# In-projection of a convolution layer by halves of the tokens instead of all at once: gate weights loaded twice, two quarters normalised in between

## The chip, the core and the metric

One core of a Trainium2 chip runs the whole program. It has a tensor engine (PE, with its weight loads as PEld), a vector engine (DVE), a scalar engine (ACT), GpSimd (POOL) and a queue that issues loads (SP). Each engine works through its own instructions in the order in which the program issued them, and waits at semaphores for others. The metric is the device time of one execution in microseconds (us).

## The reference, cut to what matters

One inference step over 1024 prompt tokens and 8 sample tokens, 1024 features, two layers. The change touches the first half of layer 0, a pair of convolutions:

```
up = rmsnorm(hp, g[0])                       # over 1024 features of each token
a_val, a_gate, b_x, b_gb, b_gc = split_cols(up @ w_in, [512, 512, 512, 512, 512])
ga = a_val * sigmoid(a_gate)                 # A: 31-tap depthwise convolution over tokens
ya = silu(layernorm(dwconv_valid(ga, a_w) + a_b, a_ln_g, a_ln_b))
zb = b_gc * b_x                              # B: 3-tap convolution
yb = b_gb * dwconv_valid(zb, b_w)
y = concatenate([ya, yb]) @ w_out
hp = hp + rmsnorm(y, g[1])                   # post-norm, then pre-norm and the MLP
```

Behind it come the MLP, the attention layer and a second MLP, none of which the change touches.

## The kernel before, in words

Features lie on partitions and tokens on the free axis. Tokens come in blocks of 512, 256 and 264 (`BW`): block 0 is the first half, blocks 1 and 2 the second. For the input norm block 0 is taken as two quarters of 256 tokens, and blocks 1 and 2 are the third and the fourth quarter (`quarters`).

All products run in a split form: a float32 operand x is kept as h, its rounding to the type fp32r, and l = x - h. ACT casts h, DVE (or POOL) subtracts l (`split_later`). A product takes three matmuls: h with h, h with l, l with h (`project`). A weight tile of 128 output columns is loaded as `raw`, 512 KB, and split into two tiles `w` (`Weights.split`); eight slices of 128 features make 24 matmuls per tile and block. `net.splitter` is the engine that subtracts: POOL from the start of the convolution layer until the first half is projected, then None, which stands for DVE; the first weights of each list go to DVE in any case.

The norm of a quarter (`normaliser`): ACT squares pieces of x, DVE adds them up (`total`), PE sums over partitions with a matrix of ones (`st`, a float32 matmul that the trace shows as two instructions), ACT takes the root, DVE refines it in three `newton` steps. Then `scaled`, for each of eight slices: DVE multiplies x by gain and root (`norm`, into PSUM), ACT casts `xh`, DVE subtracts `xl`.

The first convolution, A: for each of four chunks c of 128 channels, `glu` projects the gate g and the value v, ACT takes the sigmoid into `ga`, DVE multiplies by v. When a pair of chunks is there for a half, the task `taps` runs 31 taps for each on DVE (`taps` in PSUM in the first half, `cv` in SBUF in the second). `norm` is the layer norm behind it, whose first ones matmul is `mean`. The second, B: `conv_b(hf, c)` projects three tiles (x, c, b), and DVE and ACT do the three taps on `z`. When all of B and the layer norm of a half are there, `half` projects it with the output weights `woc` (`mm<-ybh` and `mm<-yah`), post-norms it (`y`), and pre-norms it for the MLP. These tasks run beside the main order; the MLP of the first half begins when its `xn` is there and the main order has ended the layer.

What stands in which order on an engine is decided when the program is built: the main order in `conv_layer` issues matmuls, a planner (`Pace`) keeps an estimate of each engine's time, and tasks (norms, splits, taps, half) issue their next instructions when that estimate has passed their due time. `pace.wait` lets tasks run until a condition holds. `Weights` keeps the load order (`weight_order`); `limit` is how many tiles may be loaded ahead, `ahead` how many may be split ahead of the one in use.

The main order before: chunks 0 and 1 of A for each of the four quarters in turn, the weights held; then chunks 2 and 3 of A for all three blocks; then B of the first half; then B of the second half.

Of the kernel before, what the change touches and what calls it, by code (L numbers as in the profile page):

```python
# [22 lines left out]
NB = 3  # L23
OFF = (0, 512, 768)
BW = (512, 256, 264)
KP = (2, 4, 4)
HALVES = ((0,), (1, 2))
# [28 lines left out]
LN_EXP = "natural_log_exp_and_others"  # L56
# [170 lines left out]
class Weights:  # L227
# [30 lines left out]
    def split(self, i, x, n):  # L258
        net = self.net
        yield net.pace.ready(x) + 0.1  # L260
        while i - self.taken >= self.ahead:
            yield net.pace.now() + 0.3
        h = yield from net.unit_later("w", F32R, self.back)
        l = yield from net.unit_later("w", F32R, self.back)
        yield from net.split_later(h[:, :n], l[:, :n], x[:, :n], net.splitter if i > 1 else None)
        net.free(x)
        self.whole -= 1
        self.cut.add(i)
        self.ready[i] = (h, l)
# [105 lines left out]
class Net:  # L375
# [31 lines left out]
    def weight_order(self):  # L407
        io = self.io
        main, back = [], []
        wic = lambda *cs: main.extend((io["wic"][c], 1024) for c in cs)  # L410
        wic(4, 0, 5, 1, 6, 2, 7, 3)
        for _ in range(2):
            for c in range(4):
                wic(8 + c, 16 + c, 12 + c)
        for i in range(2):
            for hf in range(2):
                for ch in range(NF // 4):
                    if i and hf and 0 < ch < NF // 4 - 1:
                        w = lambda r, c: io["w1"][i, 4 * ch + 2 * r:4 * ch + 2 * r + 2, :, c * 512:(c + 1) * 512]
                        main.append((tuple(w(r, c).rearrange("f p c -> p f c") for r in range(2) for c in range(2)), 1024))  # L420
                    else:
                        main.extend((io["w1"][i, 4 * ch + f], 1024) for f in range(4))
                    main.extend((io["w2"][i, 4 * ch + f], 1024) for f in range(4))
        for hf in range(2):
            back.extend((io["woc"][c], 1024) for c in range(KD))
        for hf in range(2):
            back.extend((io["wv"][j], 4 * NW) for j in range(2))
            back.extend((io["wia"][c], 1024) for c in (4, 0, 1, 2, 3, 11, 5, 6, 7, 8, 12, 9, 10))
            back.extend((io["woa"][c], 768) for c in range(KD))
        return main, back  # L430
# [92 lines left out]
        yield self.pace.soon()  # L523
        (engine or self.dve).tensor_sub(l, x, raw(h))

    def rstd(self, r, total, n, w, urgent, follows=LN_EXP):
        if urgent:
            bank = yield from self.bank_later("st")
            ps = bank[:, :w]
            self.pe.matmul(ps, lhsT=self.ones, rhs=total[:, :w], start=True, stop=True)  # L530
        else:
            u = yield from self.unit_later("st", F32R)
            parts = u[:, :w], u[:, SMALL:SMALL + w]
            yield from self.split_later(*parts, total[:, :w])
            yield self.pace.soon()
            bank = yield from self.bank_later("st")
            ps = bank[:, :w]
            for i in range(2):
                self.pe.matmul(ps, lhsT=self.ones_r, rhs=parts[i], start=i == 0, stop=i == 1)
            self.free(u)  # L540
        r = r[:, :w]
        self.table(LN_EXP)
        yield self.pace.soon()
        self.table(LN_EXP)
        self.act.activation(r, ps, AF.Ln, bias=self.eps, scale=1.0 / n)
        self.act.activation(r, r, AF.Exp, scale=-0.5)
        at = self.pace.soon()
        self.table(follows)
        yield at
        t = self.tmp(w, name="newton")  # L550
        self.dve.scalar_tensor_tensor(t, ps, float(n * EPS), r, ALU.add, ALU.mult)
        self.dve.scalar_tensor_tensor(t, t, -0.5 / n, r, ALU.mult, ALU.mult)
        self.dve.scalar_tensor_tensor(r, t, 1.5, r, ALU.add, ALU.mult)
        self.banks.give(bank)

    def normaliser(self, x, n, w):

        total = yield from self.small("total")
        m = x[0].shape[1]
        view = lambda t: t[:, :m * w].rearrange("p (m t) -> p m t", m=m)  # L560
        self.act.square(view(total), x[0])
        before = None
        for a in x[1:]:
            s = yield from self.small("sq")
            self.act.square(view(s), a)
            at = self.pace.soon()
            if before is not None:
                self.dve.tensor_add(view(total), view(total), view(before))
                self.drop(before)
            before = s  # L570
            yield max(at - 0.5, self.pace.calm())
        yield at
        self.dve.tensor_add(view(total), view(total), view(before))
        self.drop(before)
        if m == 2:
            self.dve.tensor_add(total[:, :w], total[:, :w], total[:, w:2 * w])
        yield self.pace.ready(total)
        r = yield from self.small("rstd")
        yield from self.rstd(r, total, n, w, self.urgent)
        self.drop(total)  # L580
        return r

    def root(self, sums, urgent):
# [432 lines left out]
    def conv_layer(self, post, first_done):  # L1016
        pace, io, sm, W = self.pace, self.io, self.small_const, self.W
        xn = [None] * NB
        quarters = [(0, slice(0, 256)), (0, slice(256, 512)), (1, slice(0, 256)), (2, slice(0, 264))]
# [21 lines left out]
            xl.append(self.feat(b, KD, "xl", F32R))  # L1041
        sa_unit, sb = self.unit("sa"), self.const.tile([P, 4, NS, 2], F32, name="sb")
        sa = sa_unit[:, :4 * NS * 30].rearrange("p (c b j) -> p c b j", c=4, b=NS)
        self.pool.dma_start(out=sa, in_=io["sa"])
        self.pool.dma_start(out=sb, in_=io["sb"])
        normed = []

        scaling = []

        def norm_in(i):  # L1050
            b, c = quarters[i]
            w = c.stop - c.start
            while i > 1 and len(scaling) < i:
                yield pace.now() + 0.2
            yield pace.ready(*x[i].tiles) if i else 0.0
            r = self.normaliser(self.pieces(x[i]), 1024, w)
            r = yield from r
            while i == 1 and not normed:
                yield pace.now() + 0.2
            scaling.append(i)  # L1060
            parts = yield from self.scaled(x[i], xh[b], xl[b], range(KD), 0, r[:, :w], c)
            self.drop(r)
            yield from self.all(parts)
            self.free(*x[i].tiles)
            normed.append(c)
# [213 lines left out]

        pace.spawn(half(0))  # L1280
        ws = []
        for i, quarter in enumerate(quarters):
            pace.wait(lambda: len(normed) > i)
            for c in range(2):
                if i == 0:
                    ws += [W.get(), W.get()]
                    W.limit = 3
                    W.ahead = 2
                glu(c, *quarter, ws[2 * c], ws[2 * c + 1], i == 0)
        for w in ws:  # L1290
            W.done(w)
        for c in (2, 3):
            wg, wv = W.get(), W.get()
            for b in range(NB):
                glu(c, b, slice(0, BW[b]), wg, wv)
            W.done(wg)
            W.done(wv)
        for hf in range(2):
            for c in range(4):
                conv_b(hf, c)  # L1300
            for b in HALVES[hf]:
                self.free(*xh[b].tiles, *xl[b].tiles)
            self.splitter = None
            projected[hf] = True
        self.pool.dma_start(out=io["o_bp"], in_=tail)
        self.pool.dma_start(out=io["o_bs"], in_=new_bs)
# [710 lines left out]
def build(tc, io):  # L2017
    with ExitStack() as ctx:
        ctx.enter_context(tc.manual_schedule())
        net = Net(ctx, tc, io)  # L2020
        net.attn_setup()
        res = [net.dr.tile([P, KD * T], F32, name=f"res{i}") for i in range(3)]
        xn = [[None] * NB for _ in range(3)]
        net.conv_layer(net.junction(1, 2, io["x"], res[0], xn[0]), lambda: xn[0][0])
        net.operands(xn[0], 0)
        net.back = BACK
        net.pace.spawn(net.carry_caches())
        gate = lambda b: xn[0][2] if b == 0 else xn[2][0]
        after = [net.junction(3, 4, res[0], res[1], xn[1], gate), net.junction(7, None, res[2], io["o_y"], None)]
        join = net.junction(5, 6, res[1], res[2], xn[2], summed=True)  # L2030
        net.urgent = False
        for hf in range(2):
            net.mlp(hf, xn[0], after[0])
            net.pace.spawn(net.attn(hf, xn[1], join))
        for hf in range(2):
            end = net.mlp(hf, xn[2], after[1], hf == 1, hf == 1)
        net.pace.wait(lambda: end.done)
# [114 lines left out]
```

## Time and profile before

| | us |
|---|---|
| median of 3 runs | 2199.3 (2199.19 to 2201.35) |
| the profiled execution | 2196.17 |
| its span in the profile | 2194.4 |

The profile is of one execution, which lies 3.1 us below the median; its span leaves 1.8 us of that execution outside. All stretches below are counted from the start of the span. A matmul's duration in the trace is modelled and overlaps its neighbours, so the pace of matmuls is read from the distance between the events that they release. PEclk is the granted clock of PE as a share of full speed (2.4 GHz); half of it is 1.2 GHz.

### The profile page before, as it was taken

The numbers are of one execution on the slowest core, as the hardware profiler recorded it, in microseconds if no ns is written. First come the engines' busy times: TensorE is split into PE (matmuls) and PEld (weight loads), VectorE is DVE, ScalarE is ACT, GpSimd is POOL, SyncE is SP. The second block draws the span as 40 slices with busy tenths as digits, with TensorE's granted clock in tenths as the row PEclk, the third lists the DMA queues.
The fourth block names the chain that finished last, engine by engine and source line by source line (L and its number), as shares of the span: only waits on it lengthen the run. The fifth ranks groups of instructions, "written<-read, shape, count | busy, mean of one in ns | idle before, by whom it ended". The sixth has DMA issues, their size and how long they took to land. (4 is left out here: it accounts for less than half of the span.)

```text
span 2194.4 us, 35516 instructions
## 1 busy us (share of the span) xinstructions
PE 2147.5 (98%) x13895; PEld 1947.7 (89%) x13895; DVE 1566.1 (71%) x2889; ACT 1113.2 (51%) x2245; POOL 149.9 (7%) x256
## 2 busy tenths in 40 slices
PE   5999999999999999999999999999999999999997
PEld 4987898889888998999989989988887989999997
DVE  8886588984764756788649575767876487777756
ACT  6125344345453643788555364356875455545434
POOL 2132010010000011000000001201000000000000
PEclk9999999999999999999999999999999999999999
DMA  4112544353533345233343343433333344232241
GB/s 180 49 58 96 166 177 157 96 173 97 174 106 117 125 154 168 85 107 119 117 142 125 123 143 124 156 121 129 103 104 125 122 166 143 107 118 86 87 140 55
DMA packets 88616, 271.04 MB, mean 124 GB/s; under 512 B 16937, under 2 KB 19129, under 8 KB 88265
## 3 DMA queue, kind: packets, MB, share of 16 engines
q1 hardware_dynamic: 77744, 223.70, 31.0%
q0 software_dynamic: 10704, 45.08, 5.4%
q8 instruction: 109, 1.79, 0.3%
q14 instruction: 59, 0.48, 0.1%
HBM read 235.41 MB, written 45.37 MB: 128 GB/s over the span
## 5 line engine op out<-in xcount | busy, mean ns | idle before, releaser
L77 PE MATMUL mm<-xh,w 128*128 128x264 f32 (+2 forms) x4208 | 997.4, 325 | 3.8 <-DVE xl L77 3.1
L77 PEld LDWEIGHTS mm<-xh,w 128*128 128x128 f32 x4208 | 710.4, 189 | 69.6 <-DVE xl L77 3.3
L77 PE MATMUL mm<-hid,w 128*128 128x264 f32 (+2 forms) x4608 | 750.7, 321 | 0.0
L77 PEld LDWEIGHTS mm<-hid,w 128*128 128x128 f32 x4608 | 658.1, 188 | 65.2 <-issue 2.7
L77 PE MATMUL mm<-xl,w 128*128 128x264 f32 (+2 forms) x2104 | 678.7, 323 | 0.0
L77 DVE TENSOR_TENSOR w<-raw,w 128x1024 fp32r<-128x1024 f32 (+1 forms) x348 | 418.5, 1210 | 173.7 <-ACT w L77 173.1
L77 ACT CAST w<-raw 128x1024 fp32r<-128x1024 f32 (+1 forms) x368 | 375.0, 1035 | 153.8 <-DMA raw<-w 58.6
L77 PEld LDWEIGHTS mm<-xl,w 128*128 128x128 f32 x2104 | 398.4, 189 | 31.3 <-issue 1.0
L77 DVE TENSOR_TENSOR acc<-acc,mm 128x256 f32<-128x256 f32 (+2 forms) x336 | 164.4, 508 | 98.8 <-PE mm L77 97.2
L77 ACT ACTIVATE relu<-mm 128x256 f32<-128x256 f32 (+2 forms) x192 | 87.3, 455 | 266.3 <-PE mm L77 238.8
L77 DVE TENSOR_TENSOR hid<-mm,hid 128x256 fp32r<-128x256 f32 (+2 forms) x192 | 97.8, 513 | 136.2 <-ACT hid L77 135.2
L77 ACT ACTIVATE mm<-relu 128x256 f32<-128x256 f32 (+2 forms) x192 | 88.8, 462 | 6.1
L77 ACT ACTIVATE hid<-relu 128x256 fp32r<-128x256 f32 (+2 forms) x192 | 91.3, 475 | 0.0
L77 DVE SCALAR_TENSOR_TENSOR cv<-ga,small,cv 128x512 f32<-128x512 f32 x120 | 83.3, 746 | 0.0
L77 DVE SCALAR_TENSOR_TENSOR taps<-ga,small,taps 128x482 f32<-128x482 f32 (+29 forms) x120 | 78.7, 734 | 0.0
L77 PE MATMUL mm<-xt,w 128*128 128x264 f32 x576 | 73.6, 284 | 0.7 <-DVE w L77 0.7
L77 PEld LDWEIGHTS mm<-xt,w 128*128 128x128 f32 x576 | 71.3, 188 | 1.3 <-DVE w L77 1.3
L77 ACT COPY qk<-mm 128x512 f32<-128x512 f32 (+2 forms) x39 | 17.4, 447 | 106.2 <-PE mm L77 101.3
L77 ACT COPY y<-mm 128x512 f32<-128x512 f32 (+2 forms) x48 | 21.5, 447 | 91.6 <-PE mm L77 91.6
L77 DVE TENSOR_TENSOR sq<-sq 128x264 f32<-128x264 f32 (+2 forms) x84 | 43.2, 514 | 30.6 <-ACT sq L77 29.7
L77 PE MATMUL mm<-mixh,w 128*128 128x512 f32 (+2 forms) x288 | 64.9, 320 | 0.0
L77 ACT CAST ph<-pt 128x512 fp32r<-128x512 f32 (+1 forms) x80 | 41.2, 523 | 34.8 <-PE pt L77 32.3
(259 smaller groups left out, 2288.6 us busy)
## 6 DMA issues: line engine op xcount, KB each, us to landing
raw<-w SPq DMA_DIRECT2D x256, 512.0 KB, 3.9
raw<-wic SPq DMA_DIRECT2D x32, 512.0 KB, 4.6
raw<-wia SPq DMA_DIRECT2D x26, 512.0 KB, 3.6
res<-res SPq DMA_DIRECT2D x18, 512.0 KB, 4.6
raw<-woc SPq DMA_DIRECT2D x16, 512.0 KB, 3.7
o_d_s<-c_d POOLq DMA_DIRECT2D x8, 1023.5 KB, 17.3
qscr<-qk POOLq DMA_DIRECT2D x26, 256.0 KB, 2.3
res<-y POOLq DMA_DIRECT2D x12, 512.0 KB, 3.8
```

Of the source, the lines that this page charges most:

```text
L77: r = fn(*args, **kw)
```

## The change

The main order now runs chunks 0 and 1 of A for the first two quarters, chunks 2 and 3 of A for block 0, B of the first half; then all four chunks of A for blocks 1 and 2, and B of the second half. The eight weight tiles of A are thus loaded and split twice. No weights are split ahead until the first two quarters have been issued (`ahead` is 0, then 0, then 2). The third and fourth quarters begin their norm only when `later` is set, behind the first two quarters. The second quarter's sum of squares is made on PE alone: two ones matmuls for each squared piece (`pe_normaliser`). DVE splits the first four weights instead of two. POOL stays the splitter through the second half's projection. Attention's constants are set up after the convolution layer is issued.

```diff
@@ Weights.split
-        yield from net.split_later(h[:, :n], l[:, :n], x[:, :n], net.splitter if i > 1 else None)
+        yield from net.split_later(h[:, :n], l[:, :n], x[:, :n], net.splitter if i > 3 else None)
@@ weight_order
-        wic(4, 0, 5, 1, 6, 2, 7, 3)
         for _ in range(2):
+            wic(4, 0, 5, 1, 6, 2, 7, 3)
             for c in range(4):
                 wic(8 + c, 16 + c, 12 + c)
@@ rstd
-        if urgent:
+        if bank is not None:
+            ps = bank[:, :w]
+        elif urgent:
@@ new
+    def pe_normaliser(self, x, n, w):
+        bank = yield from self.bank_later("st")
+        for i, a in enumerate(x):
+            s = yield from self.small("sq")
+            self.act.square(s[:, :2 * w].rearrange("p (m t) -> p m t", m=2), a)
+            yield self.pace.soon()
+            for m in range(2):
+                self.pe.matmul(bank[:, :w], lhsT=self.ones, rhs=s[:, m * w:(m + 1) * w], start=i + m == 0,
+                               stop=i == len(x) - 1 and m == 1)
+            self.drop(s)
+        r = yield from self.small("rstd")
+        yield from self.rstd(r, None, n, w, True, bank=bank)
+        return r
@@ conv_layer, norm_in
-            while i > 1 and len(scaling) < i:
+            while i > 1 and (len(scaling) < i or not later):
                 yield pace.now() + 0.2
             yield pace.ready(*x[i].tiles) if i else 0.0
-            r = self.normaliser(self.pieces(x[i]), 1024, w)
-            r = yield from r
+            r = yield from (self.pe_normaliser if i == 1 else self.normaliser)(self.pieces(x[i]), 1024, w)
@@ conv_layer, main order
-        for i, quarter in enumerate(quarters):
+        for i, quarter in enumerate(quarters[:2]):
             pace.wait(lambda: len(normed) > i)
             for c in range(2):
                 if i == 0:
                     ws += [W.get(), W.get()]
                     W.limit = 3
-                    W.ahead = 2
+                    W.ahead = 0
                 glu(c, *quarter, ws[2 * c], ws[2 * c + 1], i == 0)
+            W.ahead = 2 * i
         for w in ws:
             W.done(w)
-        for c in (2, 3):
-            wg, wv = W.get(), W.get()
-            for b in range(NB):
-                glu(c, b, slice(0, BW[b]), wg, wv)
-            W.done(wg)
-            W.done(wv)
+        later.append(True)
+        self.pool.dma_start(out=sa, in_=io["sa"])
+        self.pool.dma_start(out=sb, in_=io["sb"])
         for hf in range(2):
+            for c in (range(4) if hf else (2, 3)):
+                wg, wv = W.get(), W.get()
+                for b in HALVES[hf]:
+                    pace.wait(lambda: len(normed) > b + 1)
+                    glu(c, b, slice(0, BW[b]), wg, wv)
+                W.done(wg)
+                W.done(wv)
             for c in range(4):
                 conv_b(hf, c)
             for b in HALVES[hf]:
                 self.free(*xh[b].tiles, *xl[b].tiles)
-            self.splitter = None
+            self.splitter = None if hf else self.splitter
             projected[hf] = True
@@ build
-        net.attn_setup()
         res = [net.dr.tile([P, KD * T], F32, name=f"res{i}") for i in range(3)]
         xn = [[None] * NB for _ in range(3)]
         net.conv_layer(net.junction(1, 2, io["x"], res[0], xn[0]), lambda: xn[0][0])
+        net.attn_setup()
```

The order in which instructions stand on an engine shows three places. First, PE at the very start of the program, before the change (`st` are ones matmuls, `mm` projections; xN is a count of like rows):

```order
L2148 UNCONDITIONAL_BRANCH
L77 MATMUL st<-total,ones 128x256 x2
L77 MATMUL mm<-xh,w 128x256
L77 MATMUL mm<-xl,w 128x256
L77 MATMUL mm<-xh,w 128x256 x2
L77 MATMUL mm<-xl,w 128x256
```

and with the change:

```order
L2165 UNCONDITIONAL_BRANCH
L77 MATMUL st<-total,ones 128x256
L77 MATMUL st<-sq,ones 128x256 x8
L77 MATMUL mm<-xh,w 128x256
L77 MATMUL mm<-xl,w 128x256
```

The second quarter's single `st` on DVE's total has become eight on ACT's squares, still ahead of the first projection.

Second, PE where the third quarter's `st` stands. Before, it is inside the first quarter's projection, 58 matmuls behind the start:

```order
L77 MATMUL mm<-xl,w 128x256
L77 MATMUL mm<-xh,w 128x256
L77 MATMUL st<-total,ones 128x256
L77 MATMUL mm<-xh,w 128x256
L77 MATMUL mm<-xl,w 128x256
```

With the change it stands behind both quarters' chunks 0 and 1, three matmuls into the gate of chunk 2:

```order
L77 MATMUL mm<-xh,w 128x256
L77 MATMUL mm<-xh,w 128x512
L77 MATMUL mm<-xl,w 128x512
L77 MATMUL mm<-xh,w 128x512
L77 MATMUL st<-total,ones 128x256
L77 MATMUL mm<-xh,w 128x512
```

Third, DVE where the adds of that quarter stand (`ga` is the product of gate and value). Before, they are among the norms of the second quarter:

```order
L77 SCALAR_TENSOR_TENSOR norm<-x,small,rstd 128x256 x2
L77 TENSOR_TENSOR total<-total,sq 128x512
L77 SCALAR_TENSOR_TENSOR norm<-x,small,rstd 128x256
L77 TENSOR_TENSOR total<-total,sq 128x512 x2
L77 TENSOR_TENSOR total<-total 128x256
```

With the change they stand behind three of the four products of the first two quarters and among the first taps:

```order
L77 TENSOR_TENSOR xl<-norm,xh 128x256 x3
L77 TENSOR_TENSOR ga<-mm,ga 128x256 x3
L77 TENSOR_SCALAR taps<-ga,small 128x512 x2
L77 SCALAR_TENSOR_TENSOR taps<-ga,small,taps 128x482 x2
L77 TENSOR_TENSOR total<-total,sq 128x512
L77 SCALAR_TENSOR_TENSOR taps<-ga,small,taps 128x483
L77 TENSOR_TENSOR total<-total,sq 128x512
L77 SCALAR_TENSOR_TENSOR taps<-ga,small,taps 128x483
L77 SCALAR_TENSOR_TENSOR taps<-ga,small,taps 128x484
L77 TENSOR_TENSOR total<-total,sq 128x512
L77 TENSOR_TENSOR total<-total 128x256
```

The third product in that row needs the last matmul of the second quarter.

## Rows read from the trace of the kernel before

**Rows 1.** The page: the span, and GB/s moved in 40 equal slices of it

```profile
span 2194.4 us, 35516 instructions
...
GB/s 180 49 58 96 166 177 157 96 173 97 174 106 117 125 154 168 85 107 119 117 142 125 123 143 124 156 121 129 103 104 125 122 166 143 107 118 86 87 140 55
```

**Rows 2.** Waits of PE in the whole span: us in total, times, longest

```profile
PE st L77 <- DVE total L77: 25.6, 3, 13.3
```

**Rows 3.** Timeline of PE, 0 to 60 us: start, length, instruction, idle before

```profile
9.86 1.19 PE L77 MATMUL st<-total,ones 128*128 128x256 f32 x2 [9.86 <-DVE total L77]
24.39 1.22 PE L77 MATMUL st<-total,ones 128*128 128x256 f32 x2 [13.34 <-DVE total L77]
25.05 0.78 PE L77 MATMUL mm<-xh,w 128*128 128x256 f32 x1
...
42.29 0.39 PE L77 MATMUL mm<-xh,w 128*128 128x256 f32 x1 [3.08 <-DVE xl L77]
```

**Rows 4.** Windows: busy PE, PEld, DVE, ACT, POOL; then granted clock, DMA, GB/s

```profile
43.00:50.00 7.00, 6.14 (x28) 5.66 (x27) 6.90 (x18) 5.92 (x12) 0.00 (x0) 0.51 0.18 73
```

**Rows 5.** Timeline of DVE, 0 to 52 us

```profile
12.85 1.23 DVE L77 TENSOR_TENSOR w<-raw,w 128x1024 fp32r<-128x1024 f32 x1 [0.16 <-ACT w L77]
13.99 0.42 DVE L77 SCALAR_TENSOR_TENSOR newton<-st,rstd 128x256 f32<-128x256 f32 x1
...
15.36 1.68 DVE L77 SCALAR_TENSOR_TENSOR norm<-x,small,rstd 128x256 f32<-128x256 f32 x4
...
21.05 2.82 DVE L77 TENSOR_TENSOR total<-total,sq 128x512 f32<-128x512 f32 x1
...
26.04 1.08 DVE L77 TENSOR_TENSOR xl<-norm,xh 128x256 fp32r<-128x256 f32 x3
...
30.41 1.48 DVE L77 TENSOR_TENSOR total<-total,sq 128x512 f32<-128x512 f32 x2
```

**Rows 6.** Timeline of POOL, 0 to 52 and 50 to 260 us

```profile
18.08 5.24 POOL L77 TENSOR_TENSOR w<-raw,w 128x1024 fp32r<-128x1024 f32 x2 [13.43 <-ACT w L77]
...
79.70 4.77 POOL L77 TENSOR_TENSOR w<-raw,w 128x1024 fp32r<-128x1024 f32 x2 [40.58 <-ACT w L77]
```

**Rows 7.** Timeline of ACT, 0 to 52 and 50 to 260 us

```profile
14.07 1.13 ACT L77 ACTIVATE sq<-x 128x512 f32<-128x512 f32 x2
...
61.05 0.38 ACT L77 ACTIVATE ga<-mm 128x256 f32<-128x256 f32 x1 [3.19 <-PE mm L77]
66.74 0.38 ACT L77 ACTIVATE ga<-mm 128x256 f32<-128x256 f32 x1 [5.30 <-PE mm L77]
...
132.10 0.59 ACT L77 COPY z<-mm 128x512 f32<-128x512 f32 x1 [6.27 <-PE mm L77]
...
148.66 0.59 ACT L77 COPY z<-mm 128x512 f32<-128x512 f32 x1 [3.73 <-PE mm L77]
```

**Rows 8.** Timeline of DVE, 50 to 300 us

```profile
81.62 10.42 DVE L77 SCALAR_TENSOR_TENSOR taps<-ga,small,taps 128x496 f32<-128x496 f32 x16
...
140.22 1.54 DVE L77 SCALAR_TENSOR_TENSOR z<-z,small 128x512 f32<-128x512 f32 x2 [0.86 <-ACT z L77]
...
178.71 5.05 DVE L77 TENSOR_TENSOR total<-total,sq 128x512 f32<-128x512 f32 x2
...
254.44 0.69 DVE L77 SCALAR_TENSOR_TENSOR newton<-st,rstd 128x512 f32<-128x512 f32 x1 [2.54 <-ACT rstd L77]
...
287.75 0.68 DVE L77 TENSOR_TENSOR total<-total,sq 128x512 f32<-128x512 f32 x1
```

**Rows 9.** Timeline of PE, 150 to 320 us

```profile
169.98 1.02 PE L77 MATMUL mean<-total,ones 128*128 128x512 f32 x2
...
183.81 1.12 PE L77 MATMUL st<-total,ones 128*128 128x512 f32 x2 [2.37 <-DVE total L77]
...
202.15 0.50 PE L77 MATMUL mm<-ybh,w 128*128 128x512 f32 x1 [1.16 <-ACT w L77]
...
316.66 0.39 PE L77 MATMUL mm<-xl,w 128*128 128x512 f32 x1
```

More of the change, by code (lines that the diff above doesn't have):

```diff
@@ L524, in split_later, with rstd @@
         (engine or self.dve).tensor_sub(l, x, raw(h))
-    def rstd(self, r, total, n, w, urgent, follows=LN_EXP):
-        if urgent:
+    def rstd(self, r, total, n, w, urgent, follows=LN_EXP, bank=None):
+        if bank is not None:
+            ps = bank[:, :w]
+        elif urgent:
             bank = yield from self.bank_later("st")
@@ L1043, in conv_layer @@
         sa = sa_unit[:, :4 * NS * 30].rearrange("p (c b j) -> p c b j", c=4, b=NS)
[L1044 to L1048, printed above, removed]
+        normed, scaling, later = [], [], []
         def norm_in(i):
```

## The prediction

> **What bounds the kernel now.** I read the page first: the tensor engine (PE) is busy nearly all of a span of 2194.4 us [rows 1], so a change can gain only what PE idles, or spends at its lower clock, in the stage that is touched. PE's waits come next: the one large entry is the ones matmul `st`, which sums squares over partitions, waiting for DVE's `total`, 25.6 us in 3 waits [rows 2]. The timeline of PE shows where [rows 3]. PE runs its queue in order. The `st` of the second quarter stands ahead of the first projection, so PE waits 13.34 us for it, and projects only from 25.05. It then runs out of normalised columns and idles 3.08 us up to 42.29; over the next 7 us the granted clock is 0.51, its lower level of 1.2 GHz [rows 4], which costs half of that, 3.5 us.
>
> DVE shows why it was late [rows 5]: one add of squares takes 2.82 us where two in a row take 1.48 otherwise, because POOL splits two weights from 18.08 on [rows 6].
>
> For the rest I need PE's steps. Between the two sigmoids at 61.05 and 66.74 pass 48 matmuls of 256 columns: 5.69/48 = 0.1186 us each; 72 of 512 columns pass between the z copies at 132.10 and 148.66: 0.230 [rows 7]. 264 columns I scale to 0.121. From the mean's matmul at 169.98 to the MLP's first at 316.5 [rows 9] pass 146.5 us. The order has 291, 288 and 288 matmuls of 512, 256 and 264 columns there and four ones matmuls of about 0.86: 139.6 us. So 6.9 us are lost, at the waits of 2.37 and 1.16 us and a lower clock behind the second.
>
> **The change: the start.** The first quarter's `newton` still starts at 13.99, since its loads don't move; loads on POOL's queue only trade the mask for an earlier `sa`. Squares of the second quarter start at 14.07 [rows 7]; each now feeds two ones matmuls. Eight of these at 0.65 us or more (24.39 to 25.05, [rows 3]) hold PE to about 20; cold or warm that is hidden, since DVE is later. From 15.36 DVE has eight norms of 0.42, eight `xl` of 0.36, two weight splits of 1.23 (POOL's before) and three newton steps, 1.4 together [rows 5]: 3.4+2.9+2.5+1.4 = 10.2, so 25.5, and the last four `xl` come in one run, the first of them at 24.3. From there PE has 168 matmuls to the end of quarter two, 19.9 us: **E = 44.3**. The second quarter's own norms (6.7 us more on DVE, to 32.2) are hidden behind the first quarter's matmuls, which end at 32.9. Before, the same matmuls ended at 58.0: the sigmoid at 61.05 follows 24 matmuls of the third quarter, 2.85 us, and a hop of 0.2 [rows 7]. So 13.7 us are won here. Upper bound: PE idles 1.4 us ahead of 24.3, and a drop of clock as at 43 to 50 adds 3.
>
> **The change: what the wait turns into.** DVE has nothing to do from 32.2 to E, and behind its three `ga` products the order puts the first taps ahead of the third quarter's adds; PE has that quarter's `st` after only three matmuls of the next group. So PE stands at E+0.7 until DVE has done, from E: one product 0.4, two scalings 1.5, five taps 3.3 (0.65 each, [rows 8]), three adds of 0.6, 1.8, one half add 0.4: E+7.4. That is the lower bound. POOL meanwhile splits four weights from about E+0.3, 2.4 each (4.77 for two, [rows 6]). At 21.05 and again at 178.71 an add stood until POOL's instruction ended, each of the two at 178.71 once (5.05 us, [rows 8]), while sixteen taps, whose sum is in PSUM, kept their step of 0.65 beside a split at 79.70. So the three adds end at 5.7, 8.7 and 11.7, and `st` runs at **E+12.1**. I take this end.
>
> By the Trainium skill, page "SBUF — State Buffer", section "SBUF: two separate sides", a DVE instruction with two SBUF inputs and a GpSimd one that reads SBUF exclude each other for a whole instruction. The rows above agree; by sharing of bandwidth instead, the sum would be nearer E+7.4.
>
> After 11 idle us I expect the lower clock as after 42.29, 3 us lost (0 to 3.5). The fourth quarter's `st` follows 54 matmuls later: 12.1+12.5+0.4+3 = E+28.0. DVE has its adds done at E+27, so no wait.
>
> **The change: the way back.** From there 327 matmuls of 512 columns and 243 narrow ones bring PE to the mean: 75.5+29.0+0.4 = 104.9, so E+132.9 = 177.2. DVE's side: 120 taps and four scalings 81, third and fourth quarters' norms, splits, adds 20, gates 3, four B chunks at about 3.2, layer-norm adds 1.8: 118.6; ACT waits of 0.86 per chunk [rows 8] and one copy, 5; locks 5 at the first adds and some 4 later: E+132. The two meet, no wait (0 to 5). Behind the mean the changed order leaves 192, 336 and 381 matmuls and three ones matmuls: 133.6 us. Losses at layer norm and the first output weights stay: their chain is as before, 6.9.
>
> **Weights and POOL's queue.** Eight more loads of 512 KB: the queues moved 49 and 58 GB/s in the two slices of 55 us where they fall, 180 in the first [rows 1]; 4.2 MB over 110 us add 38: nothing. Eight more casts on ACT lie beside matmuls of 5.7 us per weight, splits of 2.4 on POOL likewise. But POOL now also splits the second half's weights, behind its stores of `y`, and in the first half's post-norm and pre-norm DVE adds with two SBUF inputs. In the changed order the pre-norm's `st` comes 24.6 us of matmuls after the post-norm's (90 and 108 narrow ones and 0.9), before 39.3. DVE took 34 us from `newton` at 254.44 to the last add at 287.75 [rows 8], with six splits (7.3) and some 5 us of B work that are no longer in it: 22 plus 2.5 for the root. Equal, so any lock is a wait: I take 2 us (0 to 9). Setting up attention later costs nothing; its constants are needed only after the MLP.
>
> **Sum.** 177.2+133.6+6.9+2 = 319.7 against 316.5: **+3.2 us**. From there PE's work is the same. On the profiled execution, 2196.17, that is 2199.4; the median shown, 2199.3, lies 3.1 above that execution, so I expect **2202**. 0.2%, what a measurement can tell here, is 4.4 us.
>
> **Rivals.**
> *No change* (forecast): what the start wins, 13.7 us, is paid back at the third quarter's `st`, 11.4 us of standing and 3 of clock, and the rest later. For it: PE's order and DVE's. 0.42.
> *Faster*: the stand at `st` is the lower bound, E+7.4, because the adds slip between POOL's instructions: 4.7 us less for PE and DVE alike; and the extra 2 us and part of the 6.9 fall away too, since the first half's projection is done long before layer norm needs PE. 2202-4.7-2-3 = 2192. For it: the first POOL split could come after the first add, were ACT's casts late. Against it: 21.05 and 178.71. 0.24.
> *Slower*: POOL's splits in the second half lock DVE between the two `st` of the first half's post- and pre-norm. Three or four of its splits fall there; each can hold an add or a scaling by 2 us: 6 us beyond the 2 taken, 2208. It decides when the last add comes over 25 us after the post-norm's `st`. For it: before, no split ran on POOL there, and DVE's chain has no slack. Against it: conv taps no longer share DVE. 0.28.
> *The start isn't earlier*: the ones matmuls stay cold to 22 and the clock drops in the gap ahead of 24.3, so that E is 49 and the gain there 9: 2207. Against it: DVE is the later one at the start. 0.06.
>
> **Numbers.** Faster 0.24, same 0.42, slower 0.34. The forecast alone spans 2195 to 2204. To leave out no more than 0.1 on a side the range goes to 2190 and 2212: below, E+7.4 with no later wait at all; above, E+3 with 7 us of locks.
>
> **What would show it.** Right: first projection near 20, quarter two's last matmul at 44 to 47; a wait of PE for `total` of 7 to 12 us right behind, with adds of over 2 us beside POOL's splits and a lower clock after it; the mean at 175 to 180; the MLP's first matmul at 317 to 322. Wrong, if PE doesn't wait there, or if the MLP starts on another side of 312 to 327; a large effect behind the MLP's start, where I expect none, would be a step that I have not seen.

## The result and the profile after

The changed kernel is slower: 2215.8 us (median of 5, 2210.9 to 2217.0) against 2199.2 (2195.1 to 2201.4), a ratio of 1.0072 with an interval of 1.0057 to 1.0087. The forecast was 2202 with a range up to 2212.

The span and PE's waits of the changed kernel, us in total, times, longest:

```profile
core 0 of [0], span 2215.0 us
...
PE st L77 <- DVE total L77: 21.3, 3, 10.8
PE mm L77 <- POOL w L77: 5.3, 3, 3.1
PE mm L77 <- DVE w L77: 4.6, 6, 1.4
PE mm L77 <- DVE ybl L77: 3.4, 1, 3.4
```

Its wait for `total` is 4 us shorter than in [rows 2], others are new; with the small ones that are left out here PE's waits grew by some 5 us, yet the span by 20.6 [rows 1]. So more than waits has to be looked for. The timeline of PE, of the changed kernel:

```profile
10.80 1.19 PE L77 MATMUL st<-total,ones 128*128 128x256 f32 x2 [10.80 <-DVE total L77]
13.86 6.74 PE L77 MATMUL st<-sq,ones 128*128 128x256 f32 x16 [1.87 <-ACT sq L77]
...
20.25 0.47 PE L77 MATMUL mm<-xh,w 128*128 128x256 f32 x1
...
44.70 0.50 PE L77 MATMUL mm<-xh,w 128*128 128x512 f32 x1 [1.07 <-ACT w L77]
48.53 0.79 PE L77 MATMUL mm<-xh,w 128*128 128x512 f32 x1 [3.10 <-POOL w L77]
55.04 1.22 PE L77 MATMUL st<-total,ones 128*128 128x256 f32 x2 [5.72 <-DVE total L77]
...
176.87 1.02 PE L77 MATMUL mean<-total,ones 128*128 128x512 f32 x2
...
264.02 0.51 PE L77 MATMUL mm<-xh,w 128*128 128x256 f32 x2 [1.62 <-POOL w L77]
276.03 2.08 PE L77 MATMUL st<-total,ones 128*128 128x512 f32 x2 [4.75 <-DVE total L77]
...
295.03 0.39 PE L77 MATMUL mm<-xh,w 128*128 128x264 f32 x1 [3.36 <-DVE ybl L77]
...
325.76 0.39 PE L77 MATMUL mm<-xl,w 128*128 128x512 f32 x1
...
351.23 2.82 PE L77 MATMUL mm<-hid,w 128*128 128x512 f32 x11 [1.29 <-DVE w L77]
...
363.73 11.60 PE L77 MATMUL mm<-hid,w 128*128 128x512 f32 x42 [1.38 <-DVE w L77]
```

Against [rows 3] PE projects from 20.25 in place of 25.05, and the second quarter ends at 43.6. Then come three waits in a row. The mean is at 176.87, 6.9 later than in [rows 9]; the MLP's first products, at 325.76, are 9.1 later. Behind the mean there is nothing above 0.6 us up to 264, then two waits of the first half's post- and pre-norm (264.02, 276.03), one for a bank that DVE empties for convolution B (295.03), and waits for the weights behind the hidden layer (`hid`).

The clock beside some of the waits is seen in windows (busy PE, PEld, DVE, ACT, POOL; then granted clock, DMA share, GB/s):

```profile
47.30:61.00 13.70, 6.75 (x15) 5.00 (x16) 13.56 (x18) 3.57 (x6) 6.68 (x3) 0.50 0.04 14
276.00:279.40 3.40, 3.37 (x9) 2.34 (x10) 0.00 (x0) 1.23 (x2) 0.00 (x0) 0.50 0.00 0
296.50:299.90 3.40, 3.40 (x18) 3.40 (x17) 3.40 (x7) 1.51 (x4) 0.00 (x0) 0.50 0.26 54
364.80:368.20 3.40, 3.40 (x10) 2.62 (x9) 3.40 (x6) 1.47 (x2) 0.00 (x0) 0.51 0.40 164
1467.30:1474.10 6.80, 6.80 (x30) 4.72 (x29) 4.87 (x16) 5.11 (x19) 0.00 (x0) 0.50 0.31 98
```

The clock fell to 0.50 (1.2 GHz), as in [rows 4], within the stand at 44 to 55, then right behind the waits that end at 276 and 295, and behind the smaller ones that end at 363.73. In the first row PE is busy for only 6.75 of the 13.7 us, so the lower clock costs about half of that there, 3.4 us; the rest PE stood anyway. The last row lies in the attention layer, where PE had waited only 0.56 us, at 1463.06; the kernel before has the same short wait.

To see where the loss is taken, ACT's `relu` of the first MLP serve as milestones: the first (counted 0), number 4, which stands behind the first accumulation over `hid`, and numbers 100 to 108, which enclose the attention layer's stretch. From number 4 to 100 all kernels here take 946.7 to 948.5 us, and from 108 to the last one 642.5 to 643.3.

| trace | median us | relu 0 | relu 4 | 100 to 108 |
|---|---|---|---|---|
| before | 2199.2 | 322.2 | 366.7 | 212.4 |
| changed | 2215.8 | 333.2 | 381.8 | 216.8 |

Of the 20.6 us of span 11.0 are lost up to relu 0, another 4.1 up to relu 4, and 4.4 in attention. The profiled execution of before was 3 us below its median, so 16.6, the difference of the medians, is the better figure for the whole.

DVE of the changed kernel, at the third quarter's adds and between post-norm and pre-norm of the first half, and POOL beside it:

```profile
46.76 2.27 DVE L77 TENSOR_TENSOR total<-total,sq 128x512 f32<-128x512 f32 x1
...
49.58 2.20 DVE L77 TENSOR_TENSOR total<-total,sq 128x512 f32<-128x512 f32 x1
...
247.15 0.69 DVE L77 SCALAR_TENSOR_TENSOR newton<-st,rstd 128x512 f32<-128x512 f32 x1 [3.25 <-ACT rstd L77]
...
259.51 1.23 DVE L77 TENSOR_TENSOR y<-y,res 128x1024 f32<-128x1024 f32 x1
...
261.99 2.53 DVE L77 SCALAR_TENSOR_TENSOR y<-y,small,rstd 128x512 f32<-128x512 f32 x1
264.56 3.46 DVE L77 TENSOR_TENSOR y<-y,res 128x1024 f32<-128x1024 f32 x1
...
268.28 5.17 DVE L77 TENSOR_TENSOR total<-total,sq 128x512 f32<-128x512 f32 x4
...
283.08 2.37 DVE L77 SCALAR_TENSOR_TENSOR z<-sb,small,z 128x8 f32<-128x8 f32 x1
285.37 0.68 DVE L77 SCALAR_TENSOR_TENSOR newton<-st,rstd 128x512 f32<-128x512 f32 x1
286.09 2.36 DVE L77 SCALAR_TENSOR_TENSOR newton<-newton,rstd 128x512 f32<-128x512 f32 x1
```

```profile
43.79 10.19 POOL L77 TENSOR_TENSOR w<-raw,w 128x1024 fp32r<-128x1024 f32 x4 [41.20 <-ACT w L77]
...
261.58 2.38 POOL L77 TENSOR_TENSOR w<-raw,w 128x1024 fp32r<-128x1024 f32 x1
...
264.53 2.40 POOL L77 TENSOR_TENSOR w<-raw,w 128x1024 fp32r<-128x1024 f32 x1
...
268.88 2.41 POOL L77 TENSOR_TENSOR w<-raw,w 128x1024 fp32r<-128x1024 f32 x1
...
282.53 2.90 POOL L77 TENSOR_TENSOR w<-raw,w 128x1024 fp32r<-128x1024 f32 x1 [1.21 <-ACT w L77]
...
285.51 5.20 POOL L77 TENSOR_TENSOR w<-raw,w 128x1024 fp32r<-128x1024 f32 x2
```

Beside each split shown an instruction of DVE that reads two tensors from SBUF is long: the scaling at 261.99 took 2.53 where others took 0.74, `y<-y,res` 3.46 where others took 1.23, one of the four adds from 268.28 2.79 in place of 0.69, and an update of eight columns 2.37 in place of 0.22. The newton step at 285.37, whose `st` is in PSUM, took its usual 0.68; the next, from SBUF alone, 2.36.

### The profile page after: what moved, and what is told of

Read it like the earlier page. It is cut to its first block, busy times and chain, and to the rows that moved or that the text cites. A ratio compares the mean times of both kernels' runs of the same rounds, so it can differ in the third digit from the quotient of the medians.

```text
span 2215.0 us, 35628 instructions
## 1 busy us (share of the span) xinstructions
PE 2162.1 (98%) x13909; PEld 1955.5 (88%) x13909; DVE 1575.2 (71%) x2870; ACT 1124.6 (51%) x2256; POOL 206.4 (9%) x279
## 5 line engine op out<-in xcount | busy, mean ns | idle before, releaser
L77 DVE TENSOR_TENSOR w<-raw,w 128x1024 fp32r<-128x1024 f32 (+1 forms) x333 | 399.7, 1208 | 154.9 <-ACT w L77 154.0
L77 ACT CAST w<-raw 128x1024 fp32r<-128x1024 f32 (+1 forms) x376 | 382.1, 1034 | 147.8 <-DMA raw<-w 62.8
L77 POOL TENSOR_TENSOR w<-raw,w 128x1024 fp32r<-128x1024 f32 x43 | 108.6, 2537 | 124.7 <-ACT w L77 102.2
L77 DVE TENSOR_TENSOR sq<-sq 128x264 f32<-128x264 f32 (+2 forms) x84 | 52.1, 620 | 53.2 <-ACT sq L77 52.4
```

The source lines that it names most:

```text
L77: r = fn(*args, **kw)
```

## The experiments

**Undo the splitter (e1).** Theory A: POOL's splits in the second half lock DVE, and everything late there follows.

```diff
-            self.splitter = None if hf else self.splitter
+            self.splitter = None
```

> The changed kernel with one line undone: POOL stops splitting weights when the first half is projected, and DVE splits the second half's weights, as before the change. Theory A (POOL's splits lock DVE's instructions with two SBUF inputs in the second half, so that the post-norm and pre-norm of the first half and then the MLP's weights come late): PE's waits for total at 276 and for ybl at 293 (4.75 and 3.4 us) fall under 3 us together, the two spells of half clock behind them go, the MLP starts 6 us sooner than at 325.7 and has no wait for its hid weights; 2202 to 2206 us. Rival B (the new order simply leaves DVE too little time between the two st, whoever splits): DVE takes the splits over at 1.23 each, the waits stay at 6 us or more, and the time stays at 2211 to 2217. Rival C (the cache copies that now start behind the MLP's start hold its weights up): the second-half waits may fall but the MLP's waits of 3 us with their lower clock stay; about 2209.

2198.5 us (10 runs), ratio 0.9997 (0.9987 to 1.0007): the whole loss is gone, more than theory A forecast. From 60 to 420 us PE waits four times in this run (the fourth is 0.52, at 208.53):

```profile
150.18 0.51 PE L77 MATMUL mm<-xh,w 128*128 128x256 f32 x2 [0.65 <-POOL w L77]
...
207.28 0.50 PE L77 MATMUL mm<-ybh,w 128*128 128x512 f32 x1 [1.30 <-ACT w L77]
...
347.95 10.96 PE L77 MATMUL mm<-hid,w 128*128 128x512 f32 x46 [1.25 <-DVE w L77]
```

A window over both norms of the first half shows PE without a pause at full clock:

```profile
230.00:330.00 100.00, 100.00 (x664) 91.52 (x663) 75.80 (x117) 45.45 (x73) 13.53 (x37) 1.00 0.55 188
```

Relu 0 comes at 318.5, 3.7 sooner than before the change, though the stand at 44 to 60 is still there. So the loss hangs on this line. It changes two things, though: POOL's work beside DVE, and the order, for the planner counts DVE's splits and puts the pre-norm's `st` 37.2 us behind the post-norm's (258.46 to 295.67), where it stood 31.5 behind with 6.4 of waits in them (244.58 to 276.03). e8 tests the first with the order kept.

**Splits ahead from the start (e2).** The waits of 1.07 and 3.10 us for chunk 2's weights were not in the prediction.

```diff
-                    W.ahead = 0
+                    W.ahead = 2
...
-            W.ahead = 2 * i
```

> The changed kernel, but weights are split up to two tiles ahead from the start on, so that POOL splits the gate and value weights of chunk 2 while the first two quarters are projected and not at their end. Theory A: the waits of 1.07 and 3.10 us for those weights go, the first add of the third quarter no longer stands beside a split, so that its st comes at about 7.4 us behind the end of the second quarter's projection in place of 11.4, and the spell of half clock shrinks from 13.7 to under 7 us; the mean comes 6 to 9 us sooner than at 176.9, of which the second half's locks may take some back; 2206 to 2212 us. Rival B (DVE's order alone sets the st): the wait moves wholly into the st, which stays near 11 us behind, and the time stays within 2 us of the changed kernel.

2204.0 us, ratio 1.0031 (1.0015 to 1.0046), below theory A's 2206 to 2212. The stand is gone. DVE of this run:

```profile
46.95 0.79 DVE L77 TENSOR_TENSOR total<-total,sq 128x512 f32<-128x512 f32 x1
...
48.29 0.68 DVE L77 TENSOR_TENSOR total<-total,sq 128x512 f32<-128x512 f32 x1
...
49.52 0.68 DVE L77 TENSOR_TENSOR total<-total,sq 128x512 f32<-128x512 f32 x1
```

With POOL's split over at 47.2 the adds take 0.68 to 0.79, and `st` runs at 50.8, 7 us behind the second quarter's end, by now with 30 matmuls of chunk 2 ahead of it; PE does not wait. But the mean stays at 177.2, and not 6 to 9 us sooner as theory A has it, and what PE won comes back in part: it waits 6.24 us for `total` at 289. By the ratios 9 us are gained on the changed kernel. Of the 12.9 us that this trace's span is shorter 6.1 show at relu 0, 2.3 more up to relu 4, and 4.2 are the attention layer's clock, which was full in this trace.

**Norm of the last quarters later (e3).**

```diff
-        later.append(True)
...
+            later.append(True)
             for c in range(4):
                 conv_b(hf, c)
```

> The changed kernel, but the third and fourth quarters may begin their norm only when chunks 2 and 3 of the first half have been issued, so that the st of the third quarter no longer stands three matmuls behind the first two quarters on PE. Theory A (that st alone makes PE stand there): the wait of 5.7 us for total and the long spell of half clock go, the two waits for weights (4.2 us) stay; the mean comes about 9 us sooner; 2204 to 2209 us. Rival B (DVE's chain of taps, norms and layer norm sets the first half's out-projection anyway): PE's gain is given back as a wait at the layer norm's mean or st near 170 to 185, and the time stays within 2 us of the changed kernel.

2217.4 us, ratio 1.0085 (1.007 to 1.010). The wait of 5.7 us went, and the mean came at 176.0, 0.9 sooner and not 9: rival B in the time, though PE gives its gain back ahead of the mean and not at it. PE got small waits for the late `total` and `xl` (1.1, 2.0, 2.5), and 6.12 us for the pre-norm's `total` at 287.8.

**No cache copies (e6).** Leaves out the copies of the cache to its outputs.

```diff
-        net.pace.spawn(net.carry_caches())
```

> The changed kernel without the copies of the cache (some 8 MB that POOL's queue starts at 333 to 338 us, and more later); the cache outputs are left out, so only the stretch around the MLP's start is to be read. Theory A (DVE is late there, so that the hid weights are split and their raw slots freed late): PE still waits 2 to 3 us for hid weights at 350 to 365. Rival C (the copies slow the loads of the weights): those waits go, and the MLP's first accumulation comes 4 to 6 us sooner against its start.

2211.6 us, ratio 1.0059 (1.0042 to 1.0075), an interval that overlaps the changed kernel's. The wait of 1.38 us at 364 and with it 2.8 of the 4.1 us between relu 0 and 4 are gone; one wait of 1.30 for a weight and 0.48 for `hid` stay. What the copies could hold up is the load of the MLP's weights, which ACT waits for; of the changed kernel:

```profile
359.56 2.00 ACT L77 CAST w<-raw 128x1024 fp32r<-128x1024 f32 x2 [9.93 <-DMA raw<-w]
```

The kernel before waits 4.68 us at this cast, and e6 not at all. That the 2.8 us are the copies' is not shown: e5 below has the copies, waits 7.58 us at the cast, and loses still less between relu 0 and 4 (45.0 us, e6 45.8, before 44.5). In both runs the order on DVE differs from the changed kernel's in one split near 340, which stands one tap sooner.

**Both edits (e7).** e1 and e2 together.

> The changed kernel with both earlier edits: DVE splits the second half's weights, and weights are split two tiles ahead from the start. Theory A (two separate losses, each from POOL's splits beside DVE's instructions): the gains add up; against the run with DVE's splits alone, where PE lost 9.9 us of waits and 7 us at the lower clock between 43 and 60, PE now loses under 4 us there, so that the MLP starts 8 to 13 us sooner than the 312 us or so of that run; 2184 to 2191 us, under the kernel before. Rival B (DVE is then the bound of the layer norm or the pre-norm): the early gain comes back as waits for total between 170 and 300, and the time stays at 2194 to 2199.

2207.4 us, ratio 1.0046 (1.0033 to 1.0060): worse than e1 alone, and above both ranges. Rival B is the nearer one, but the waits are for weights and `xl`, not for `total`. PE of this run:

```profile
320.48 0.80 PE L77 MATMUL mm<-xh,w 128*128 128x512 f32 x1 [5.39 <-DVE xl L77]
```

Up to 60 PE loses nothing, but the mean stands at 185.4 as in e1 (184.2), since DVE's taps end no sooner; the out-projection begins at 219.4 in place of 207.3, behind more of the second half's matmuls, and in the end PE has done all of the second half and stands for the first half's columns. With waits of 2.12 and 3.18 us and three spells of half clock from 221 us on, the start's gain is more than paid back. That the planner's order does this is read from the trace and was not tried by itself.

**POOL repeats the splits for nobody (e8).** e1, and behind each of DVE's splits of the second half POOL subtracts once more, into the raw tile that is dead by then.

```diff
+        if net.extra is not None:
+            net.nc.gpsimd.tensor_sub(x[:, :n], x[:, :n], raw(h[:, :n]))
         net.free(x)
...
-            self.splitter = None if hf else self.splitter
+            self.splitter, self.extra = None, True if hf == 0 else None
```

> The changed kernel with DVE splitting the second half's weights, and POOL repeating each of those subtractions into the raw tile that is dead by then: the order on PE and DVE is that of the run with DVE's splits alone, PE waits for none of POOL's results, only the raw slots come free later. Theory A (a POOL instruction with SBUF inputs holds DVE's, whoever needs its result): DVE's adds and scalings take 1.8 to 2.5 us beside them, PE waits for total or ybl again for 6 us or more in the second half, and the time is 2208 to 2220. Rival B (what cost was that PE's weights stood behind stores in POOL's queue, or the z copies behind the splits): DVE's durations stay at 0.7, and the time is within 4 us of 2198.5.

2216.0 us, ratio 1.0084 (1.0070 to 1.0098): by the ratios (1.0084 less 0.9997) 19 us above e1, with the same order on PE, DVE and ACT, for work that PE does not wait for. DVE, POOL and PE of this run:

```profile
273.39 3.30 DVE L77 TENSOR_TENSOR y<-y,res 128x1024 f32<-128x1024 f32 x1
...
312.54 0.68 DVE L77 SCALAR_TENSOR_TENSOR newton<-st,rstd 128x512 f32<-128x512 f32 x1
313.25 1.84 DVE L77 SCALAR_TENSOR_TENSOR newton<-newton,rstd 128x512 f32<-128x512 f32 x1
315.13 2.76 DVE L77 SCALAR_TENSOR_TENSOR rstd<-newton,rstd 128x512 f32<-128x512 f32 x1
```

```profile
273.20 2.40 POOL L267 TENSOR_TENSOR raw<-raw,w 128x1024 f32<-128x1024 f32 x1 [1.16 <-DVE w L77]
...
311.23 6.11 POOL L267 TENSOR_TENSOR raw<-raw,w 128x1024 f32<-128x1024 f32 x2
```

```profile
306.15 1.56 PE L77 MATMUL st<-total,ones 128*128 128x512 f32 x2 [4.16 <-DVE total L77]
321.99 0.38 PE L77 MATMUL mm<-xh,w 128*128 128x256 f32 x1 [2.73 <-DVE xl L77]
```

So POOL's instructions by themselves bring such a loss: two newton steps beside two of them take 4.6 us in place of 1.4, and PE waits even where the order leaves DVE 37 us. The 19 us are no price of the lock in the changed kernel, though, since DVE does the splits here as well; what the order alone would cost without the lock was not tried. The raw slots and POOL's stores and copies, which come later here too, are not kept apart; from 180 to 382 us neither PE nor DVE shows a wait for a result of POOL.

By the Trainium skill, page "SBUF — State Buffer", section "SBUF: two separate sides", whichever of the two starts first has the shared ports for its whole instruction, and the other blocks fully. The rows agree for the case that POOL is first (261.58 and 261.99), down to the newton step from PSUM beside its neighbours from SBUF.

**The line alone on the kernel before (e9).** POOL stays the splitter, all else is as before.

> The kernel before with one line of the change alone: POOL stays the splitter through the second half's projection. Theory A: the same lock in the same stage; DVE's last add before the pre-norm st (288.4 before) comes later than the st's place on PE (about 293), PE waits 2 to 6 us there and the hid weights come late; 2203 to 2213 us. Rival B (only the changed order leaves the second half too little time): no wait, 2197 to 2201 us.

2212.1 us, ratio 1.0065 (1.0051 to 1.0079). One line makes nine tenths of the change's loss. As in e1 it also moves the order: between the two `st` lie 30.2 us of PE's work in place of 39.4, since the planner no longer counts splits on DVE. PE waits at the same `st`:

```profile
289.47 2.07 PE L77 MATMUL st<-total,ones 128*128 128x512 f32 x2 [5.67 <-DVE total L77]
```

Relu 0 is at 332.3, as in the changed kernel (333.2).

**Attention's set-up back (e5).** The two lines in `build` undone.

> The changed kernel with attention's constants set up first, as before the change. Forecast: no difference from the changed kernel, 2211 to 2217 us. Rival C (the set-up, which stood on POOL at 331 to 333 ahead of the cache copies, moves the copies into the loads of the MLP's weights): the waits for hid weights at 350 to 365 go, about 2209. Also read: whether the spells of half clock near 1467 and 1498 us, which cost 4 us in the changed kernel's trace, are there again.

2213.2 us, ratio 1.0074 (1.0060 to 1.0087), no difference from the changed kernel in time. In the trace the wait of 1.38 us at 364 is gone as in e6; the first wait (1.29) is there. The spells near 1467 and 1497 are there too, and two more: 220.0 from relu 100 to 108.

**The start alone on the kernel before (e10).** `pe_normaliser` for the second quarter, and DVE splits the first four weights.

> The kernel before with the start of the change alone: the second quarter's squares summed on PE, and DVE splitting the first four weights. Theory (the second quarter's st no longer waits for DVE's adds; PE was the bound up to the MLP): PE projects from 20 in place of 25.05, the wait of 13.34 us falls to about 2; DVE is later by two splits (2.5 us) for the third and fourth quarters, so that of 5 us some 3 stay; 2193 to 2198 us. Rival (DVE sets the projection until about 50): PE waits for xl instead, and the time stays at 2196 to 2201.

2198.8 us, ratio 0.9997 (0.9988 to 1.0006). The wait of 13.34 us fell to 3.65, but PE stands 4.16 us at 31.8 for `xl`, and relu 0 is at 321.8, 0.4 sooner than before: the rival, DVE is the bound of the start. The lock has a part in it: the norm ahead of that `xl` took 2.65 us, beside a split on POOL from 28.77.

**No split on POOL at all (e12 on the kernel before, e13 on the changed one).** `self.splitter` is None from the start.

> The kernel before with all weights split by DVE and none by POOL. Theory A (a split on POOL costs DVE more than the split itself where DVE has adds with two SBUF inputs, less where it has taps on PSUM): the adds at 21.05 and 178.71 take 0.7 each, but DVE gains 16 or so splits of 1.23 in the first 200 us; about no change, 2195 to 2203 us. Rival (POOL's help is needed in the first half, where DVE has its taps): the layer norm comes 10 us or more later than at 170, and the time is above 2205.

> The changed kernel with all weights split by DVE and none by POOL. Theory A for the stand at the third quarter's st: its adds take 0.7 in place of 1.6 to 2.3, but DVE now has the splits of chunk 2's weights there too, so st comes 8 to 12 us behind the second quarter's end as in the changed kernel; the second half is as with DVE's splits there. 2200 to 2210 us, since the first half's taps now share DVE with its splits. Rival: PE waits at the layer norm for 5 us or more; above 2210.

2212.1 us, ratio 1.0053 (1.0038 to 1.0067), and 2227.4, ratio 1.0122 (1.0105 to 1.0139). The mean comes at 187.1 and 218.3, 17 and 41 us later than with POOL's help. Both times are those of the rivals, but PE does not wait at the layer norm: the planner moves it back, and PE stands for the first half further on, in e13 at the pre-norm:

```profile
331.49 2.07 PE L77 MATMUL st<-total,ones 128*128 128x512 f32 x2 [19.45 <-DVE total L77]
```

So POOL's help is worth much in the first half, where DVE's taps are in PSUM and keep their step: by the ratios 12 us in e12 against the kernel before, and 27 in e13 against e1, the planner's moves included. In the second half it does harm (e1, e9).

**The kernel before again (e14).**

> The kernel before once more, for its trace. If the spells of half clock near 1450 to 1500 us, in the attention layer, belong to the changed order, they are absent again, as in the profile shown; if they come and go from run to run, they can be there, and the stretch between the 100th and the 108th relu then takes 4 us more than 212.4.

One run, 2195.4 us; relu 100 to 108 takes 212.4 again, without a spell.

| trace | relu 0 | relu 4 | 100 to 108 |
|---|---|---|---|
| e1 DVE splits | 318.5 | 364.5 | 216.6 |
| e2 ahead | 327.1 | 373.4 | 212.6 |
| e3 late norm | 329.6 | 382.1 | 218.5 |
| e5 set-up | 334.0 | 379.0 | 220.0 |
| e6 no copies | 332.6 | 378.4 | 216.9 |
| e7 e1 and e2 | 328.1 | 372.5 | 216.6 |
| e8 POOL extra | 334.6 | 382.5 | 216.6 |
| e9 before, POOL | 332.3 | 377.2 | 216.7 |
| e10 start | 321.8 | 366.4 | 218.4 |
| e12, e13 no POOL | 334.2, 350.0 | 378.7, 394.4 | 215.5, 218.3 |

No version here beats the kernel before by more than the measurement can tell.

## Why the prediction was wrong

*The start* was right: E, the end of the second quarter, was forecast at 44.3 and is 43.6, the first projection near 20. e10 shows that it is worth nothing by itself.

*What the wait turns into*: the end was right, `st` at E+11.4 where E+12.1 was forecast, with two adds of about 2.2 us beside POOL's splits, and 7 in e2 where they had none (lower bound 7.4). One thing was missed there: PE waits first for chunk 2's weights, 4.2 of the 9.9 us, as nothing is split ahead before E. The lower clock lasts 13.7 us, but with PE busy for 6.75 of them it costs 3.4, near the 3 forecast.

*The way back* was right: the mean at 176.9, forecast 177.2, with DVE's last sum for it done at 176.2. As the traces read, this is why e2, e3 and e7 gained little there: DVE's chain still ends at 174.2, 174.6 and 182.9 us, and the mean stands behind it.

*Layer norm and output weights*: 6.9 us were to be lost again "as before"; the changed kernel waits under 1 there. This step helped.

*Weights and POOL's queue* is the step that failed: "any lock is a wait: I take 2 us (0 to 9)". The mechanism was named, and its place; the size was wrong. From the post-norm's first newton step to the last add DVE took 28.8 us (247.15 to 275.97) where 22 were forecast. Three instructions held by a split make 6.1 of the 6.8 us: the scaling at 261.99 1.8, `y<-y,res` 2.2, one add 2.1. That gave the wait of 4.75. Not in the sum were the weight split behind a store of `y` (1.62), the same lock at the pre-norm's newton steps and convolution B's states (3.36 at 295.03), and the lower clock behind both, up to 1.7 each. In all 15.3 us are lost from the mean to the MLP (325.76 less 176.87 less 133.6 of work), against 8.9 forecast; with under 1 of waits at the layer norm, the term taken at 2 came to some 14. The rival *slower* had the mechanism and its three holds of 2 us, and was the right one; its 2208 stops at the pre-norm's `st` and is 8 us short.

*"From there PE's work is the same"* failed too: 4.1 us are lost at the first accumulation. No split runs on POOL there, and DVE's splits and taps keep their usual 1.22 and 0.75 us. PE waits 1.29 us for a weight that DVE splits late, as in e1, and 1.38 for one whose load ACT gets late (e6), with the lower clock behind it; what makes the difference between 4.1 us here and 0.5 in e5 was not settled. With 9.1 and 4.1 in place of 3.2 the sum would have been 2209 on the profiled execution, 2212.5 by the median; what remains to 2215.8 is of the size of the spells in attention.

## What to carry to other kernels

Price a helper engine by what it holds up: a split on POOL took 2.4 us here, and DVE instructions with two SBUF inputs that met one lost up to 2.2, more than the 1.23 that DVE needs to do the split itself. The splits on POOL paid where DVE worked from PSUM, and did harm where it worked from SBUF with no slack. When PE gains time in a stage, look whether the results that end the stage come from another engine's chain; if so, the gain can be paid back as a wait further on, and here the clock fell behind most of those waits as well.

## What was not expected of the hardware

Near 1440 to 1510 us, in the attention layer, the granted clock fell to 0.50, mostly for 6.8 and again for 3.4 us, in nearly all traces of other kernels; relu 100 to 108 then takes 215.5 to 220.0 us in place of 212.4. PE's one wait above 0.15 us in that stretch, 0.56, is in the kernel before as well. The spells were absent in both traces of the kernel before and in e2. Whether the kernel or the run decides it no trace settles, but the single runs point to the run. The ten of e1 fall into two groups: four of 2195.5 to 2197.2 us at a mean granted clock of 0.994 or 0.995, and six of 2198.4 to 2200.8 at 0.992, the traced one, with its spells, among these. Those of the kernel before lie between 2193.7 and 2205.5, wide enough for both cases.
